# Two layers of a hybrid decoder in one kernel: the stationary tiles and the split weights at other SBUF addresses

## The chip, the cores and the metric

The kernel runs on one core of a Trainium2 chip. The metric is the device time of one execution in microseconds (us). Three runs of the kernel before took 2104.9, 2106.04 and 2107.2 us; the median is 2106.04 us. TensorE, VectorE, ScalarE and GpSimd are called PE, DVE, ACT and POOL, as in the profile; SP is the queue that starts the transfers.

## The reference

The input x has 256 positions of 2048 numbers. Each of the two layers does this:

```python
h = rmsnorm(x, norm_mix)
q, k, v, u_ssm, z_u, z_v = split(h @ w_in)          # 2048 -> 2816
y_attn = sliding_window_gqa(q, k, v, attn_sinks)    # 16 heads, window of 128
y_ssm  = s5_mixer(u_ssm, ...)                       # scan over positions, then GLU
y_gmlp = gmlp_mixer(z_u, z_v, ...)                  # gating in chunks of 128
y = concat(rmsnorm(y_attn), rmsnorm(y_ssm), rmsnorm(y_gmlp))
x = x + y @ w_out                                   # 2048 -> 2048
h = rmsnorm(x, norm_ffn)
x = x + (silu(h @ w_gate) * (h @ w_up)) @ w_down    # 2048 -> 5632 -> 2048
```

and a last RMSNorm ends it. All of it is float32. The products with `w_in`, `w_out`, `w_gate`, `w_up`, `w_down` and the GLU weight are called dense here; they are nearly all of the arithmetic.

## The kernel before

**Weights.** All dense weights lie in DRAM as one list of 684 halves of 128x1024 float32 (512 KB each), in the order of their use. `pump` (line 159 issues it) loads a half into one of five `raw` buffers. `split_hi` (line 168, ACT) rounds it to a tile `whi` of the type fp32r, and `split_lo` (line 178, DVE) puts the rest, raw minus whi, into a tile `wlo`; there are four buffers of each. So every weight is whi + wlo.

**Stationary tiles.** The activations are split in the same way and held transposed, ready to be loaded into the PE array as the stationary operand. `xh` and `xl` hold the two parts of the 2048 normalised inputs (16 blocks of 128 rows by 256 positions; the pair is called X). `ya` and `yb` hold blocks 0 to 7 and 8 to 15 of the input of `w_out` and `w_down`, each with both parts inside (Y). These are the four stationary tiles, each 16 KiB in a partition.

**The product.** `unit` takes one block k and, for each half m of the positions, issues three matmuls of 512 columns into one accumulator: xh with whi (line 260), xh with wlo (line 261), xl with whi (line 262). The trace names the moving tile first: `acc<-whi,xh` has whi moving and xh stationary. Every matmul comes with its own load of 128 stationary columns (LDWEIGHTS, engine PEld). A half of the weights serves 12 matmuls. `dense` runs over the blocks; after each `unit` pair it calls `tick`, which lets the waiting small jobs (attention, state space, transposes, evictions) put their instructions between the dense ones. The trace calls their PSUM tiles `side`.

**Order.** Per layer: `w_in` from X, `w_out` and the GLU product from Y, then the feed-forward part in three sets of four, four and three column groups: `w_gate` and `w_up` from X, `w_down` from Y. In `w_down` the blocks run from ya to yb and, for the next 512 output columns, again from ya to yb. The order on every engine is written out by the program itself (`manual_schedule`); pools only give out buffers and addresses.

**Addresses.** A pool lays its tiles out in the order in which their tags first appear, one pool behind the other. `xh` and `xl` (lines 953, 954) come from the pool `const`, everything else named here from the one pool `work`. Pools decide nothing but the address: a tag keeps its number of buffers wherever it lies.

Of the kernel before, what the change touches and what calls it, by code (L numbers as in the profile page):

```python
# [1 line left out]

# [8 lines left out]
F32R = mybir.dt.float32r  # L11
# [107 lines left out]
class Split:  # L119
    def __init__(self, parts):  # L120
        self.parts = parts

    def _at(self, i, k0, k1):
        hi, lo, base = self.parts[k0 // 8 if len(self.parts) > 1 else 0]
        return (hi, lo)[i][:, k0 - base:k1 - base]
# [3 lines left out]

    def lo(self, k0, k1):  # L130
        return self._at(1, k0, k1)


class Builder:
# [811 lines left out]
    def build(self):  # L946
        nc = self.nc
        dr = self.dr
        cst = self.const
        W = self.work  # L950

        self.x = cst.tile([128, 2, 2048], F32, name="x")
        xh = cst.tile([128, 16, 256], F32R, name="xh")
        xl = cst.tile([128, 16, 256], F32R, name="xl")
        self.X = Split([(xh, xl, 0)])
        self.Y = Split([None, None])
        self.ident = cst.tile([128, 128], F32, name="ident")
# [50 lines left out]
        for l in range(L):  # L1008
# [53 lines left out]
            for t in out_tiles():  # L1062
# [12 lines left out]
                f = n not in accs  # L1075
# [80 lines left out]
        for m in range(2):  # L1156
            r = nrm["rs"][:, m:m + 1]
            t = self.work.tile([128, 2], F32, tag="ms", name="ms", bufs=4)
# [13 lines left out]
def build_program(shapes):  # L1172
    nc = bacc.Bacc("TRN2", target_bir_lowering=False, num_devices=1, dynamic_dma_scratch_size=1024)
    dr = {n: nc.dram_tensor(n, s, F32, kind="ExternalInput").ap() for n, s in shapes.items()}
    dr["out"] = nc.dram_tensor("out", (2, 128, D), F32, kind="ExternalOutput").ap()
    with tile.TileContext(nc) as tc:
        with tc.tile_pool(name="const", bufs=1) as cst, tc.tile_pool(name="work", bufs=1) as wrk, \
                tc.tile_pool(name="ps", bufs=1, space=bass.MemoryType.PSUM) as ps, \
                tc.tile_pool(name="dram", bufs=1, space=bass.MemoryType.DRAM) as dram:
            with tc.manual_schedule():  # L1180
                b = Builder(nc, tc, (cst, wrk, ps, dram), dr)
                b.build()
    return nc, b

# [11 lines left out]
```

## Time and profile before

| | |
|---|---|
| median of three runs | 2106.04 us |
| profiled execution | 2106.98 us |
| its span, first to last instruction | 2105.1 us |
| PE busy | 2076.0 us (99%) |
| loads of stationary columns (PEld) | 1708.8 us (81%) |
| DVE busy | 1213.1 us (58%) |
| ACT busy | 969.4 us (46%) |
[...]

Matmuls are pipelined and their ends are modelled, so they overlap in the trace: one of 512 columns lasts near 390 ns, but the next starts some 230 ns after it. What a matmul costs in a row of matmuls is therefore the distance between two starts, not its duration.

### The profile page before, as it was taken

The page shows a single profiled execution, that of the slowest core. Times are in us where ns is not written, and L with a number is a line of the kernel's source. Part 1 is how long each engine was busy: PE and PEld are TensorE (multiplying, and loading weights), DVE is VectorE, ACT ScalarE, POOL GpSimd, SP SyncE. Part 2 cuts the span into 40 slices and gives each one's busy share as a digit, 9 for nine tenths or more (in the row PEclk, how much of TensorE's full clock was granted, in tenths as well). Part 3 has the DMA queues.
Part 4 walks back from the last instruction along what each step waited for, and adds up shares of the span by engine and source line. Part 5 has one row for each costly group of instructions (what it writes and reads, how often), then busy time and mean ns, then how long its engine had stood idle before and what let it go on. Part 6 is the DMA issues. An engine that isn't in the chain of part 4 may idle for free.

```text
span 2105.1 us, 25614 instructions
## 1 busy us (share of the span) xinstructions
PE 2076.0 (99%) x9728; PEld 1708.8 (81%) x9728; DVE 1213.1 (58%) x1625; ACT 969.4 (46%) x1289; POOL 204.4 (10%) x196
## 2 busy tenths in 40 slices
PE   8998999999999999999999999999999999999998
PEld 7788888888888888888888888888888888888886
DVE  6998765655555555444556795554454444554445
ACT  6555554444444443344455445544443444434443
POOL 0555004031312100000000010000000000000000
PEclk9998999999999999999999999999999999999999
DMA  7433455565656565555565455555555555555554
GB/s 243 166 128 133 140 180 190 185 212 189 220 189 214 185 210 190 190 183 188 180 215 179 152 187 174 180 189 181 188 183 191 187 184 186 187 191 183 187 193 140
DMA packets 105595, 387.98 MB, mean 184 GB/s; under 512 B 12288, under 2 KB 13056, under 8 KB 104192
## 3 DMA queue, kind: packets, MB, share of 16 engines
q1 hardware_dynamic: 105472, 386.35, 54.8%
q8 instruction: 76, 1.25, 0.2%
q14 instruction: 47, 0.39, 0.1%
HBM read 375.03 MB, written 11.27 MB: 184 GB/s over the span
## 4 chain that ended last, share of the span: by engine, by line
PE 95%; DVE 3%; issue 1%; ACT 0%; DMA 0%; SPq 0%; POOLq 0%; POOL 0%; ACTq 0%
PE acc L260 29%; PE acc L261 29%; PE acc L262 29%; PE side L324 2%; PE side L834 1%; DVE wlo L178 1%; PE side L606 1%; PE side L798 1%; DVE st L614 0%; PE side L566 0%; PE side L823 0%; PE side L644 0%; PE side L642 0%; PE side L639 0%; DMA x<-x 0%
## 5 line engine op out<-in xcount | busy, mean ns | idle before, releaser
L178 DVE TENSOR_TENSOR wlo<-raw,whi 128x1024 fp32r<-128x1024 f32 (+1 forms) x687 | 857.5, 1253 | 686.9 <-ACT whi L168 685.7
L168 ACT ACTIVATE whi<-raw 128x1024 fp32r<-128x1024 f32 (+1 forms) x687 | 725.3, 1057 | 1005.5 <-PE acc L262 943.8
L260 PE MATMUL acc<-whi,xh 128*128 128x512 f32 (+1 forms) x1792 | 711.4, 397 | 1.4 <-ACT whi L168 1.4
L261 PE MATMUL acc<-wlo,xh 128*128 128x512 f32 (+1 forms) x1792 | 701.6, 392 | 0.2 <-DVE wlo L178 0.2
L262 PE MATMUL acc<-whi,xl 128*128 128x512 f32 (+1 forms) x1792 | 701.3, 391 | 0.0
L262 PEld LDWEIGHTS acc<-whi,xl 128*128 128x128 f32 x1792 | 337.5, 188 | 77.4
L260 PEld LDWEIGHTS acc<-whi,xh 128*128 128x128 f32 x1792 | 337.9, 189 | 73.5 <-ACT whi L168 1.8
L261 PEld LDWEIGHTS acc<-wlo,xh 128*128 128x128 f32 x1792 | 338.0, 189 | 73.0 <-DVE wlo L178 1.0
L260 PE MATMUL acc<-whi,ya 128*128 128x512 f32 x512 | 204.6, 400 | 0.0
L262 PE MATMUL acc<-whi,ya 128*128 128x512 f32 x512 | 202.0, 395 | 0.0
L261 PE MATMUL acc<-wlo,ya 128*128 128x512 f32 x512 | 202.0, 394 | 0.0
L260 PE MATMUL acc<-whi,yb 128*128 128x512 f32 x448 | 176.6, 394 | 0.0
L262 PE MATMUL acc<-whi,yb 128*128 128x512 f32 x448 | 174.8, 390 | 0.0
L261 PE MATMUL acc<-wlo,yb 128*128 128x512 f32 x448 | 174.5, 390 | 0.0
L298 POOL TENSOR_TENSOR rs<-ms,nh 128x2 f32<-128x2 f32 (+1 forms) x12 | 12.2, 1014 | 1532.9 <-DVE ms L297 1413.6
L262 PEld LDWEIGHTS acc<-whi,ya 128*128 128x128 f32 x512 | 96.3, 188 | 22.7
L261 PEld LDWEIGHTS acc<-wlo,ya 128*128 128x128 f32 x512 | 96.5, 189 | 21.5
L260 PEld LDWEIGHTS acc<-whi,ya 128*128 128x128 f32 x512 | 96.5, 189 | 21.3
L262 PEld LDWEIGHTS acc<-whi,yb 128*128 128x128 f32 x448 | 84.1, 188 | 18.0
L260 PEld LDWEIGHTS acc<-whi,yb 128*128 128x128 f32 x448 | 84.1, 188 | 17.1
L261 PEld LDWEIGHTS acc<-wlo,yb 128*128 128x128 f32 x448 | 84.2, 188 | 17.0
L360 DVE SCALAR_TENSOR_TENSOR xl<-side,gains,xh 128x256 fp32r<-128x256 f32 x64 | 27.9, 479 | 45.6 <-ACT xh L358 45.5
(223 smaller groups left out, 1278.0 us busy)
## 6 DMA issues: line engine op xcount, KB each, us to landing
raw<-wts SPq DMA_DIRECT2D x684, 512.0 KB, 3.8
saved<-stash SPq DMA_DIRECT2D x4, 1792.0 KB, 6.5
stash<-saved SPq DMA_DIRECT2D x3, 1792.0 KB, 7.4
stashb<-saved SPq DMA_DIRECT2D x2, 1792.0 KB, 9.4
bc<-bc SPq DMA_DIRECT2D x8, 256.0 KB, 3.5
out<-x SPq DMA_DIRECT2D x8, 256.0 KB, 3.0
saved<-stashb SPq DMA_DIRECT2D x1, 1792.0 KB, 7.4
x<-x SPq DMA_DIRECT2D x3, 512.0 KB, 8.0
```

Of the source, the lines that this page charges most:

```text
L168: self.nc.scalar.activation(out=h[:, o:o + w], in_=self.raw[j][:, o:o + w], func=AF.Copy)
L178: self.nc.vector.tensor_tensor(out=o[:, i:i + w], in0=r[:, i:i + w], in1=self.hi[j][:, i:i + w], op=ALU.subtract)
L260: nc.tensor.matmul(out=o, lhsT=a, rhs=wh, start=first, stop=False)
L261: nc.tensor.matmul(out=o, lhsT=a, rhs=wl, start=False, stop=False)
L262: nc.tensor.matmul(out=o, lhsT=b, rhs=wh, start=False, stop=last)
L298: nc.gpsimd.tensor_tensor(out=out, in0=t, in1=self.nh[:, 0:w], op=ALU.pow)
L324: nc.tensor.transpose(ps[:, 256 * kk + 128 * m:256 * kk + 128 * m + 128], parts(2 * b + kk, m), self.ident)
L360: nc.vector.scalar_tensor_tensor(out=o, in0=src, scalar=gain[:, k:k + 1], in1=h.bitcast(F32), op0=ALU.mult, op1=ALU.subtract)
L606: nc.tensor.matmul(out=ps[:, 256 * o + 64 * g:256 * o + 64 * g + 64], lhsT=st[nm][:, 128 * g:128 * g + 128], rhs=U4[:, 4 * ct + g, :])
L798: nc.tensor.matmul(out=ps[:, nk * i:nk * i + nk], lhsT=qT[:, h0 + i], rhs=self.kT[:, j, cq, 0:nk], start=(j == 0), stop=(j == 1))
L834: nc.tensor.matmul(out=ps[:, 64 * i:64 * i + 64], lhsT=pT[:, 128 * (nb * i + b):128 * (nb * i + b) + 128], rhs=self.v[:, b, 64 * cq:64 * c ...
```

## The change

`const` gives up `xh` and `xl`, and the pool `work` becomes four pools, laid out one behind the other. A class `Homes` stands in for the pool and sends each tag to its pool: first everything that is not named, then `whi` and `wlo`, then the four stationary tiles, then a few tiles of the state space and gating parts.

```diff
+class Homes:
+    TAGS = (
+        (),
+        ('whi', 'wlo'),
+        ('xh', 'xl', 'ya', 'yb'),
+        ('stash', 'S', 'U4', 'st', 'wst', 'v', 'bb'),
+    )
+
+    def __init__(self, pools):
+        self.home = {t: p for ts, p in zip(self.TAGS, pools) for t in ts}
+        self.rest = pools[0]
+
+    def tile(self, shape, dtype, tag, name, bufs=1):
+        return self.home.get(tag, self.rest).tile(shape, dtype, tag=tag, name=name, bufs=bufs)
...
-        xh = cst.tile([128, 16, 256], F32R, name="xh")
-        xl = cst.tile([128, 16, 256], F32R, name="xl")
+        xh = W.tile([128, 16, 256], F32R, tag="xh", name="xh")
+        xl = W.tile([128, 16, 256], F32R, tag="xl", name="xl")
...
-        with tc.tile_pool(name="const", bufs=1) as cst, tc.tile_pool(name="work", bufs=1) as wrk, \
...
+            cst = pool("const")
+            homes = Homes([pool(f"work{i}") for i in range(len(Homes.TAGS))])
```

The instructions, their order on each engine and the semaphores that they wait for are the same in both programs; what differs is where the tiles lie. Addresses within a partition, as the two programs have them (each matmul loads 512 bytes of its stationary tile, at a multiple of 512 bytes from the tile's start):

| tile | before, bytes | before, KiB | after, bytes | after, KiB |
|---|---|---|---|---|
| x (residual stream) | 1152 | 1.1 to 17.1 | 1152 | 1.1 to 17.1 |
| xh | 17536 | 17.1 to 33.1 | 130816 | 127.75 to 143.75 |
| xl | 33920 | 33.1 to 49.1 | 147200 | 143.75 to 159.75 |
| yb | 151552 | 148.0 to 164.0 | 163584 | 159.75 to 175.75 |
| ya | 202112 | 197.4 to 213.4 | 179968 | 175.75 to 191.75 |
| raw, five | from 57984 | 56.6 to 76.6 | from 25216 | 24.6 to 44.6 |
| whi, four | from 80640 | 78.75 to 94.75 | from 98048 | 95.75 to 111.75 |
| wlo, four | from 97024 | 94.75 to 110.75 | from 114432 | 111.75 to 127.75 |
| t4, four (small jobs) | from 113408 | 110.75 to 126.75 | from 47872 | 46.75 to 62.75 |
| stash (state space) | 181632 | 177.4 to 191.4 | 198400 | 193.75 to 207.75 |

## Rows read from the trace of the kernel before

**Rows 1.** The page: busy time and share of the span, then instructions.
```profile
PE 2076.0 (99%) x9728; PEld 1708.8 (81%) x9728; DVE 1213.1 (58%) x1625; ACT 969.4 (46%) x1289; POOL 204.4 (10%) x196
```
**Rows 2.** The page: the chain that ended last, by engine and by line.
```profile
PE 95%; DVE 3%; issue 1%; ACT 0%; DMA 0%; SPq 0%; POOLq 0%; POOL 0%; ACTq 0%
PE acc L260 29%; PE acc L261 29%; PE acc L262 29%; PE side L324 2%; PE side L834 1%; DVE wlo L178 1%; PE side L606 1%; PE side L798 1%; DVE st L614 0%; PE side L566 0%; PE side L823 0%; PE side L644 0%; PE side L642 0%; PE side L639 0%; DMA x<-x 0%
```
**Rows 3.** Busy time by stage: us, engines (instructions), granted clock, DMA share, GB/s.
```profile
60.00:250.00 190.00, 178.55 (x1005) 154.73 (x1004) 165.17 (x353) 105.34 (x202) 77.48 (x77) 0.95 0.40 139
250.00:1100.00 850.00, 850.00 (x3800) 691.81 (x3799) 461.28 (x455) 381.71 (x449) 103.42 (x95) 1.00 0.58 195
1300.00:2050.00 750.00, 750.00 (x3298) 608.65 (x3297) 371.67 (x350) 317.69 (x343) 1.60 (x1) 1.00 0.57 187
...
552.20:563.30 11.10, 11.10 (x49) 9.03 (x48) 7.51 (x7) 4.25 (x4) 6.55 (x4) 1.00 0.81 287
...
872.50:922.30 49.80, 49.80 (x216) 40.38 (x215) 24.23 (x22) 20.25 (x20) 0.00 (x0) 1.00 0.57 190
```
**Rows 4.** Instructions of PE in order, 552 to 575 us: start, duration, what.
```profile
552.19 0.40 PE L260 MATMUL acc<-whi,ya 128*128 128x512 f32 x1
...
563.12 0.40 PE L262 MATMUL acc<-whi,ya 128*128 128x512 f32 x1
563.35 0.39 PE L260 MATMUL acc<-whi,yb 128*128 128x512 f32 x1
...
574.01 0.40 PE L262 MATMUL acc<-whi,yb 128*128 128x512 f32 x1
574.24 0.40 PE L260 MATMUL acc<-whi,ya 128*128 128x512 f32 x1
```
**Rows 5.** Groups of PE, 552.20 to 563.30 us: count, busy us, mean ns.
```profile
L260 PE MATMUL acc<-whi,ya 128*128 128x512 f32 x16 | 6.3, 395 | 0.0
```
**Rows 6.** The same groups, 563.40 to 574.20 us.
```profile
L260 PE MATMUL acc<-whi,yb 128*128 128x512 f32 x16 | 6.2, 389 | 0.0
```
**Rows 7.** Instructions of PE in order, 872 to 923 us.
```profile
872.39 0.40 PE L260 MATMUL acc<-whi,xh 128*128 128x512 f32 x1
...
922.36 0.39 PE L262 MATMUL acc<-whi,xl 128*128 128x512 f32 x1
922.59 0.60 PE L324 MATMUL side<-ident,t 128*128 128x128 f32 x4
```
**Rows 8.** Groups of PE, 872.50 to 922.30 us.
```profile
L260 PE MATMUL acc<-whi,xh 128*128 128x512 f32 x72 | 28.4, 395 | 0.0
```
**Rows 9.** Instructions that read yb: duration ns min/median/max, first and last start.
```profile
L260 PE MATMUL acc<-whi,yb x448: 389/389/486, 249.7 to 2095.0; 128*128 128x512 f32 x150
L260 PE MATMUL side<-whi,yb x16: 389/389/498, 244.1 to 1279.7; 128*128 128x512 f32 x16
```
**Rows 10.** Groups of PE, 250 to 2100 us, shapes kept apart.
```profile
L260 PE MATMUL acc<-whi,xh 128*128 128x512 f32 x1568 | 625.5, 399 | 0.0
L260 PE MATMUL acc<-whi,ya 128*128 128x512 f32 x480 | 191.3, 399 | 0.0
L260 PE MATMUL acc<-whi,yb 128*128 128x512 f32 x448 | 176.6, 394 | 0.0
L324 PE MATMUL side<-ident,t 128*128 128x128 f32 x208 | 30.8, 272 | 0.0
```
**Rows 11.** Groups of PE, 0 to 250 us, shapes kept apart.
```profile
L260 PE MATMUL acc<-whi,xh 128*128 128x512 f32 x160 | 67.6, 423 | 1.4 <-ACT whi L168 1.4
L260 PE MATMUL acc<-whi,ya 128*128 128x512 f32 x32 | 13.3, 414 | 0.0
```
**Rows 12.** Groups of the whole span, shapes kept apart: mean ns, idle time before.
```profile
L178 DVE TENSOR_TENSOR wlo<-raw,whi 128x1024 fp32r<-128x1024 f32 x681 | 853.7, 1258 | 686.9 <-ACT whi L168 685.7
L168 ACT ACTIVATE whi<-raw 128x1024 fp32r<-128x1024 f32 x681 | 721.8, 1060 | 1004.6 <-PE acc L262 943.8 <-issue 30.8 <-ACT whi L168 7.7
L260 PE MATMUL acc<-whi,xh 128*128 128x512 f32 x1728 | 693.1, 401 | 1.4 <-ACT whi L168 1.4
```

More of the change, by code (lines that the diff above doesn't have):

```diff
@@ L1 @@
+import contextlib
 import math
@@ L1176, in build_program @@
     with tile.TileContext(nc) as tc:
-        with tc.tile_pool(name="const", bufs=1) as cst, tc.tile_pool(name="work", bufs=1) as wrk, \
-                tc.tile_pool(name="ps", bufs=1, space=bass.MemoryType.PSUM) as ps, \
-                tc.tile_pool(name="dram", bufs=1, space=bass.MemoryType.DRAM) as dram:
+        with contextlib.ExitStack() as st:
+            pool = lambda name, **kw: st.enter_context(tc.tile_pool(name=name, bufs=1, **kw))
+            cst = pool("const")
+            homes = Homes([pool(f"work{i}") for i in range(len(Homes.TAGS))])
+            ps = pool("ps", space=bass.MemoryType.PSUM)
+            dram = pool("dram", space=bass.MemoryType.DRAM)
             with tc.manual_schedule():
-                b = Builder(nc, tc, (cst, wrk, ps, dram), dr)
+                b = Builder(nc, tc, (cst, homes, ps, dram), dr)
                 b.build()
```

## The prediction

> **What bounds the kernel now.** I read the busy shares first: PE is busy for 2076.0 of 2105.1 us [rows 1]. A busy PE need not be a PE at its peak, so next comes the chain that ended last: 95% of it is PE, and 87% is the three dense lines [rows 2]. The stages say the same: from 250 to 1100 us and from 1300 to 2050 us PE is busy without a gap at full granted clock, while DVE stands at 54% (461.28 of 850), ACT at 45% and the transfers at 58% [rows 3]. Only before 250 us does PE wait: from 60 to 250 us it is busy for 178.55 of 190 us, DVE for 165.17 (87%), and the granted clock is 0.95 [rows 3]. So for some 1800 us the time is the number of matmuls times the distance from one start to the next, and nothing else.
>
> The third view is that distance, from instructions in order of time. In one `w_down` stage the blocks run through ya and then yb. The first ya matmul starts at 552.19 us, the first yb matmul at 563.35, the next ya matmul at 574.24 [rows 4]; between them lie 16 matmuls on each of three lines, 48 in all [rows 5, 6]. That is 11.16 us / 48 = 232.5 ns on ya and 10.89 us / 48 = 226.9 ns on yb. The instruction, its 512 columns, the moving tiles and the clock are the same; what differs is the stationary tile. X behaves like ya: from 872.39 to 922.59 us [rows 7] stand 72 matmuls on each line [rows 8], so 50.20 us / 216 = 232.4 ns. It isn't one lucky stretch: of the 448 yb matmuls of line 260 the shortest and the median last 389 ns, and the same holds for the 16 that write another PSUM tile [rows 9], while the pure stretch of X averages 395 [rows 8].
>
> Now the addresses. xh and xl lie at 17 to 49 KiB, ya at 197 to 213 KiB, yb at 148 to 164 KiB. The slow tiles lie on both sides of the fast one. Line 260, with whi moving, lasts as long over X as over ya, and yb is fast under the same moving buffers; so the moving tile doesn't make the difference. I read it as a property of where the stationary tile lies. The change puts all four between 127.75 and 191.75 KiB, and keeps whi and wlo between 64 and 128 KiB, where they are now.
>
> **The change part by part.** No instruction, order or wait is added or removed, so the sum has only durations in it.
>
> *X moves to 127.75 KiB.* After 250 us there are 1568 matmuls of 512 columns on line 260 with xh [rows 10], so 4704 on three lines. If each costs what yb's cost, the gain is 4704 x (232.4 - 226.9) = 25.9 us.
>
> *ya moves from 197 to 175.75 KiB.* 480 on line 260 after 250 us [rows 10], 1440 in all, at 232.5 - 226.9 = 5.6 ns: 8.1 us.
>
> *yb moves from 148 to 159.75 KiB.* It is fast now and stays so: 0. If it loses its place, 448 x 3 + 16 x 3 = 1392 matmuls [rows 9] pay 5.6 ns: 7.8 us lost.
>
> *Before 250 us* there are (160 + 32) x 3 = 576 such matmuls [rows 11], worth 0 to 3.2 us at 5.5 ns. DVE is the busier partner there, at 87% against 54% later, so a quicker PE mostly waits sooner; I take 1 us.
>
> *Switches.* The matmul during which a load from another place runs seems to stay slow: the last yb before ya takes 574.24 - 574.01 = 0.23 us, and so does the last xl before the transposes [rows 4, 7]. Those small jobs stay elsewhere. The 208 transposes of one kind come in fours [rows 7, 10], 52 entries at 5.5 ns: 0.3 us, for all kinds some 0.5 us off the gain.
>
> *raw, whi, wlo and the small tiles move too.* ACT's split takes 1060 ns on the mean and DVE's 1258, with 1004.6 and 686.9 us of idle time before them [rows 12]. In the trace both are spread evenly over their buffers' addresses, from 57 to 111 KiB; the new ones are not sampled. Their cover is the half's 12 matmuls: 12 x 226.9 ns = 2.72 us, against 1.26 us of DVE. Even a tenth more would hide after 250 us. So 0; in the early stage, where DVE is short, 1% on its 165.17 us [rows 3] would be 1.7 us either way. Transfers move 512 KB a half, and their share rises from 0.58 to 0.60.
>
> The sum is 25.9 + 8.1 + 1.0 - 0.5 = 34.5 us. The profiled execution took 2106.98 us, 1.9 us more than its span; less 34.5 that is 2072.5, and the median of the runs lies 0.9 us lower. I predict 2072 us.
>
> The distance between 5.0 and 7 ns bounds it from rows: with all matmuls that follow a small job counted in, line 260's mean is 399 on xh and ya against 394 on yb after 250 us [rows 10], 6144 x 5 = 30.7 us; over the whole span xh has 401 [rows 12], 7 ns above 394, and 7 x 6720 = 47 us would be the most, if each line gained like line 260 and the early waits fell as well. The clean starts lie nearer the lower end, so I keep 34.5; the forecast's own range is 2063 to 2079 us.
>
> [...]
>
> **The rivals.**
>
> *The fast place is yb's own (slower).* In this trace two properties of yb go together: it lies between 128 and 192 KiB, and it starts at 151552 bytes, a whole multiple of 4096. The three slow tiles start 128 or 384 bytes past a multiple of 512; after the change all four start 256 past one. If the fine alignment to 512 or more decides, or the exact 16 KiB, no tile is fast afterwards and yb pays its 7.8 us: 2106 + 8 = 2114 us. It decides if yb's matmuls stand at 232 ns afterwards. Against it: the new starts are multiples of 256, as yb's is and the slow ones aren't, and so only an alignment that counts from 512 bytes up, or a span narrower than the change's, would take the gain away. A chance of 0.11.
>
> *Part of the span is fast.* xh, at 127.75 to 143.75 KiB, lies wholly outside what yb has sampled. If the fast span begins at 144 KiB, two of X's three loads stay slow, and the third is between two switches, each 0.23 us [rows 4]: X gains nothing, ya gains its 8.1 us, 2098 us. If instead only the part above 164 KiB were slow, X would gain and ya not: 2080, about 2084 with half of yb's place lost. Together 0.07, spread from 2080 to 2100.
>
> *The address is invisible.* Then yb is fast because of what runs beside it. For it: the transfers ran at 287 GB/s beside ya's stretch, with POOL at work for 6.55 of 11.10 us [rows 3]. Against it: X's 216 matmuls, with POOL idle and 190 GB/s [rows 3], stand at the same 232.4 ns. 2106 us, 0.05. [...]
>
> **How the numbers follow.** Forecast 0.77, slower 0.11, part 0.07, invisible 0.05. A difference under 0.2% (4.2 us) can't be told from no change here. Faster takes the forecast and nearly all of the partial cases: 0.83; same 0.06; slower 0.11. The range takes in the forecast's own 2063 to 2079 and the better part of the partial cases: 2063 to 2090 us.
>
> **What would show it.** In the profile after, a pure stretch of X and one of ya should each show 227 ns from start to start, medians of 389 ns, and no slow matmul where ya and yb meet. The stage from 250 to 1100 us should hold the same work in some 833 us, and DVE and ACT keep 1258 and 1060 ns. The second step fails if xh is slow and ya fast (part of the span), all of it if yb reads 232 (its own place). The forecast is wrong with right reasons if the distances are 227 and PE shows new waits for whi or wlo after 250 us.

## The result, and the profile after

The changed kernel takes 2071.23 us (median of four runs, 2070.05 to 2073.87), against 2106.27 us for the kernel before (2104.9 to 2107.2). The ratio is 0.9836, with a 95% interval of 0.9819 to 0.9853: 35 us less. The forecast was 2072 us, in a range of 2063 to 2090.

The page of the changed kernel begins so; the third line answers to [rows 1].

```profile
span 2072.0 us, 25614 instructions
...
PE 2041.6 (99%) x9728; PEld 1708.3 (82%) x9728; DVE 1210.9 (58%) x1625; ACT 969.9 (47%) x1289; POOL 206.1 (10%) x196
```

The counts are those of before. The busy time that is gone is PE's: 34.4 us, where the other engines differ by 2.2 us or less, and the span is 33.1 us shorter. The chain that ended last is still PE's:

```profile
PE 94%; DVE 4%; issue 1%; ACT 0%; DMA 0%; SPq 0%; POOLq 0%; POOL 0%; ACTq 0%; DVEq 0%
```

Next the instructions of PE in order of time (start, duration, what), for the same pair of `w_down` runs as in [rows 4]. The dense lines are now 279 to 281.

```profile
547.11 0.39 PE L279 MATMUL acc<-whi,ya 128*128 128x512 f32 x1
...
557.77 0.39 PE L281 MATMUL acc<-whi,ya 128*128 128x512 f32 x1
557.99 0.39 PE L279 MATMUL acc<-whi,yb 128*128 128x512 f32 x1
...
568.65 0.39 PE L281 MATMUL acc<-whi,yb 128*128 128x512 f32 x1
568.87 0.39 PE L279 MATMUL acc<-whi,ya 128*128 128x512 f32 x1
```

The 48 matmuls on ya take 10.88 us and the 48 on yb 10.88, 226.7 ns each; ya's were 232.5 ns before. The last matmul of each run, next to the other tile, takes 0.22 us where it took 0.23. A pure stretch of X stands in the same view:

```profile
861.15 0.39 PE L279 MATMUL acc<-whi,xh 128*128 128x512 f32 x1
...
910.12 0.60 PE L343 MATMUL side<-ident,t 128*128 128x128 f32 x4
```

Between the two lie the 216 matmuls of [rows 7] and [rows 8]: 48.97 us / 216 = 226.7 ns, where it was 232.4. The instructions that read each tile (duration as min/median/max, then first and last start), which answer to [rows 9]:

```profile
L279 PE MATMUL acc<-whi,xh x1792: 278/389/794, 10.0 to 1994.5; 128*128 128x512 f32 x193, 128*128 128x256 f32 x7
...
L279 PE MATMUL acc<-whi,ya x512: 388/389/486, 213.9 to 2059.1; 128*128 128x512 f32 x171
...
L279 PE MATMUL acc<-whi,yb x448: 389/389/486, 250.0 to 2061.8; 128*128 128x512 f32 x150
```

All three tiles have the median that only yb had, 389 ns. The last column of times says where the gain lies: the first yb matmul starts at 250.0 us, after 249.7 before, so no gain shows up to there; the last one starts 33.2 us earlier. And the groups of line 279 after 250 us (count, busy us, mean ns), which answer to [rows 10], and the two splits over the whole span, which answer to [rows 12]:

```profile
L279 PE MATMUL acc<-whi,xh 128*128 128x512 f32 x1568 | 618.0, 394 | 0.0
...
L279 PE MATMUL acc<-whi,ya 128*128 128x512 f32 x480 | 188.9, 393 | 0.0
...
L279 PE MATMUL acc<-whi,yb 128*128 128x512 f32 x448 | 176.4, 394 | 0.0
```

```profile
L197 DVE TENSOR_TENSOR wlo<-raw,whi 128x1024 fp32r<-128x1024 f32 x681 | 851.7, 1255 | 658.8 <-ACT whi L187 657.9
L187 ACT ACTIVATE whi<-raw 128x1024 fp32r<-128x1024 f32 x681 | 722.4, 1061 | 969.3 <-PE acc L281 919.2 <-issue 27.8 <-ACT whi L187 8.0
```

The splits cost what they cost before (1258 and 1060 ns). Their idle time shrank by 28 and 35 us. For most of it DVE waits for ACT's part, 657.9 us where it was 685.7, and ACT for a matmul of PE, 919.2 us where it was 943.8.

### The profile page after: what moved, and what is told of

Same layout as the page of the kernel before. It is cut to its first block, busy times and chain, and to the rows that moved or that the text cites. A ratio compares the mean times of both kernels' runs of the same rounds, so it can differ in the third digit from the quotient of the medians.

```text
span 2072.0 us, 25614 instructions
## 1 busy us (share of the span) xinstructions
PE 2041.6 (99%) x9728; PEld 1708.3 (82%) x9728; DVE 1210.9 (58%) x1625; ACT 969.9 (47%) x1289; POOL 206.1 (10%) x196
## 4 chain that ended last, share of the span: by engine, by line
PE 94%; DVE 4%; issue 1%; ACT 0%; DMA 0%; SPq 0%; POOLq 0%; POOL 0%; ACTq 0%; DVEq 0%
PE acc L279 29%; PE acc L281 29%; PE acc L280 29%; PE side L343 2%; DVE wlo L197 1%; PE side L853 1%; PE side L625 1%; PE side L817 1%; DVE st L633 0%; PE side L585 0%; PE side L842 0%; PE side L663 0%; PE side L661 0%; DMA raw<-wts 0%; PE side L658 0%
## 5 line engine op out<-in xcount | busy, mean ns | idle before, releaser
L197 DVE TENSOR_TENSOR wlo<-raw,whi 128x1024 fp32r<-128x1024 f32 (+1 forms) x687 | 855.6, 1250 | 658.9 <-ACT whi L187 657.9
L187 ACT ACTIVATE whi<-raw 128x1024 fp32r<-128x1024 f32 (+1 forms) x687 | 725.8, 1058 | 971.1 <-PE acc L281 919.2
L279 PE MATMUL acc<-whi,xh 128*128 128x512 f32 (+1 forms) x1792 | 704.2, 393 | 1.9 <-ACT whi L187 1.9
L281 PE MATMUL acc<-whi,xl 128*128 128x512 f32 (+1 forms) x1792 | 693.1, 387 | 0.0
L280 PE MATMUL acc<-wlo,xh 128*128 128x512 f32 (+1 forms) x1792 | 692.6, 387 | 0.0
L279 PE MATMUL acc<-whi,ya 128*128 128x512 f32 x512 | 202.0, 394 | 0.0
L281 PE MATMUL acc<-whi,ya 128*128 128x512 f32 x512 | 199.5, 390 | 0.0
```

The source lines that it names most:

```text
L187: self.nc.scalar.activation(out=h[:, o:o + w], in_=self.raw[j][:, o:o + w], func=AF.Copy)
L197: self.nc.vector.tensor_tensor(out=o[:, i:i + w], in0=r[:, i:i + w], in1=self.hi[j][:, i:i + w], op=ALU.subtract)
L279: nc.tensor.matmul(out=o, lhsT=a, rhs=wh, start=first, stop=False)
L280: nc.tensor.matmul(out=o, lhsT=a, rhs=wl, start=False, stop=False)
L281: nc.tensor.matmul(out=o, lhsT=b, rhs=wh, start=False, stop=last)
```

## The experiments

The forecast rests on a reading: a stationary tile is quick because of the place where it lies. The theory *span* says that the place is 128 to 192 KiB. The theory *start* says that it is the start of the tile, a multiple of 256 bytes or not. The first two kernels each move one tile of 128 bytes, so that the two theories part, and the third leaves the model out.

**The stationary pair X 128 bytes later, in its old place.** In the kernel before:

```diff
+        self.sinks = cst.tile([128, L, 16], F32, name="sinks")
         xh = cst.tile([128, 16, 256], F32R, name="xh")
         xl = cst.tile([128, 16, 256], F32R, name="xl")
...
-        self.sinks = cst.tile([128, L, 16], F32, name="sinks")
```

Expected:

> The kernel before with one 128-byte tile (sinks) moved ahead of xh, so that xh and xl start 128 bytes later, at multiples of 256 bytes (17664 and 34048), still far below 128 KiB; whi, wlo, ya and yb keep their addresses. Theory span (a stationary tile is quick where it lies between 128 and 192 KiB): X stays at 232.4 ns from start to start, 2106 us. Theory start (it is quick where it starts at a multiple of 256 bytes, as yb did and the three slow tiles did not): X falls to 227 ns, 4704 x 5.5 ns = 26 us less, 2080 us.

Measured: 2078.36 us, ratio 0.9874 (0.986 to 0.9889). This is start's number and not span's. The groups of PE from 250 to 2100 us in this kernel:

```profile
L260 PE MATMUL acc<-whi,xh 128*128 128x512 f32 x1568 | 617.8, 394 | 0.0
...
L260 PE MATMUL acc<-whi,ya 128*128 128x512 f32 x480 | 191.4, 399 | 0.0
...
L260 PE MATMUL acc<-whi,yb 128*128 128x512 f32 x445 | 175.5, 394 | 0.0
```

X, at 17 KiB, is as quick as yb, 394 ns on the mean; ya, untouched, keeps its 399 ns. The span theory falls here, although its number was right.

**Everything 128 bytes earlier.** In the changed kernel:

```diff
-        ('stash', 'S', 'U4', 'st', 'wst', 'v', 'bb'),
+        ('stash', 'S', 'U4', 'st', 'wst', 'v', 'bb', 'smh'),
```

Expected:

> The changed kernel with one 128-byte tile (smh) moved from the first pool to the last, so that whi, wlo and the four stationary tiles start 128 bytes earlier: the stationary tiles lie 128 bytes off a multiple of 256 (as the slow tiles of before did), at 127.6 to 191.6 KiB. Theory span: all stay at 227 ns, 2071 us. Theory start: all four are slow at 232.4 ns, 2071 + 35 + 8 = 2114 us.

Measured: 2070.29 us, ratio 0.9839 (0.9822 to 0.9855). This is span's number and not start's. The groups of PE from 250 to 2100 us:

```profile
L279 PE MATMUL acc<-whi,xh 128*128 128x512 f32 x1568 | 617.7, 394 | 0.0
...
L279 PE MATMUL acc<-whi,ya 128*128 128x512 f32 x480 | 188.8, 393 | 0.0
...
L279 PE MATMUL acc<-whi,yb 128*128 128x512 f32 x444 | 174.8, 394 | 0.0
```

So neither theory of the stationary tile alone holds both results. What the first kernel changed and the second did not is the distance between the stationary and the moving tile: in the second, whi and wlo moved along.

**A map without the model.** The core of the kernel, with `r` the thirteen tiles ra to rm, 16 KiB each:

```python
for s in TILES:              # stationary
    for m in TILES:          # moving
        for q in range(16):
            nc.tensor.matmul(**mm(q, s, m, 0, 0, False, False))    # line 47: no offset
# lines 51, 55, 59, 63: stationary, moving, both 128 bytes late, both 256 bytes late
```

Expected:

> Nothing of the model is computed: thirteen fp32r tiles ra to rm lie at 16, 32, ... 208 KiB, each 16 KiB long, filled with part of x, and TensorE runs 16 matmuls of 512 columns for every pair of a stationary tile and a moving tile, with no other engine at work; then for 7 stationary and 5 moving tiles again with the stationary, the moving or both operands 128 bytes later, and with both 256 bytes later. Theory span: rh, ri, rj and rk (128 to 192 KiB) as stationary show about 227 ns from start to start and 389 ns of duration, all others about 232 and 393, whatever the moving tile and whatever the offset. Theory start: all tiles show 227 with no offset and with 256 bytes, and 232 where the stationary operand is 128 bytes late. A third theory, pair: what counts is the stationary tile against the moving one, and the quick pairs follow the distance between them or their 64 KiB blocks, so that 128 to 192 KiB is quick under a moving tile in 64 to 128 KiB and not under one elsewhere.

It took 1171.15 us. Busy time of PE and PEld by pass, for the lines 47, 51, 55, 59 and 63 in turn (stretch, its length, busy us and matmuls):

```profile
0.00:1169.00 1169.00, 613.08 (x2704) 507.51 (x2704) 1.00 0.01 3
0.00:1169.00 1169.00, 130.29 (x560) 105.52 (x560) 1.00 0.01 3
0.00:1169.00 1169.00, 130.82 (x560) 105.14 (x560) 1.00 0.01 3
0.00:1169.00 1169.00, 127.14 (x560) 105.11 (x560) 1.00 0.01 3
0.00:1169.00 1169.00, 127.10 (x560) 105.11 (x560) 1.00 0.01 3
```

Divided by the matmuls: 226.7 ns over all 169 pairs of places, 232.7 with the stationary operand 128 bytes late, 233.6 with the moving one late, and 227.0 with both late, by 128 or by 256 bytes. Of the 169 pairs the costliest has 3.8 us of busy time for its 16 matmuls, 389 ns each; with the moving operand 128 bytes late all 35 pairs have 3.9 us, and 394 or 395 ns each. So no span and no pair of blocks is slow. Only the third theory, pair, is left, and not in the form in which it was written: neither blocks of 64 KiB nor large distances count, but a small distance between the two operands. The map has only 0 and 128 bytes of it; that it counts modulo 256 is read from the kernel before, where yb and the first whi lie 277 x 256 bytes apart (151552 and 80640) and take 226.9 ns. Once the tiles are filled the program gives the other engines nothing to do until the last matmul, and the transfers' share is 0.01, so contention with them isn't needed for the 6 ns.

**The moving tiles alone 128 bytes earlier.** In the changed kernel:

```diff
-        ('whi', 'wlo'),
+        ('whi', 'wlo', 'smh'),
```

Expected:

> The changed kernel with the 128-byte tile smh moved behind wlo, so that whi and wlo start 128 bytes earlier while the four stationary tiles keep the addresses of the changed kernel (130816 to 196352). Theory pair (what counts is the distance between the stationary and the moving operand's start, modulo 256 bytes): all dense matmuls are slow at 232 to 234 ns, yb's too, so at least 2071 + (6720 + 1392) x 5.6 ns = 2116 us, slower than the kernel before. Theories span and start: the stationary tiles have not moved, 227 ns, 2071 us.

Measured: 2113.93 us, ratio 1.0042 (1.0026 to 1.0059): slower than the kernel before, with every stationary tile where the changed kernel has it. Groups of PE from 250 to 2100 us:

```profile
L279 PE MATMUL acc<-whi,xh 128*128 128x512 f32 x1568 | 625.5, 399 | 0.0
...
L279 PE MATMUL acc<-whi,ya 128*128 128x512 f32 x480 | 191.3, 399 | 0.0
...
L279 PE MATMUL acc<-whi,yb 128*128 128x512 f32 x441 | 175.9, 399 | 0.0
```

All three are at 399 ns, yb too. The expectation of 2116 us or more was 2 us too high; its direction and the place are right.

**The pools in another order.** In the changed kernel:

```diff
     TAGS = (
+        ('xh', 'xl', 'ya', 'yb'),
         (),
         ('whi', 'wlo'),
-        ('xh', 'xl', 'ya', 'yb'),
-        ('stash', 'S', 'U4', 'st', 'wst', 'v', 'bb'),
+        ('stash', 'S', 'U4', 'st', 'wst', 'v', 'bb', 'smh'),
     )
...
-        self.rest = pools[0]
+        self.rest = pools[1]
```

Expected:

> The changed kernel with its four pools in another order: the stationary tiles at 24.6 to 88.6 KiB, whi and wlo at 159.6 to 191.6 KiB, all of them 128 bytes past a multiple of 256, so that the distances between them are multiples of 256 bytes. Theory pair: 227 ns everywhere, 2071 us. Theory span: no stationary tile is in the quick span, 232 ns, 2114 us. Theory start (multiples of 256): 2114 us as well.

Measured: 2070.71 us, ratio 0.9836 (0.9822 to 0.9851), the changed kernel's own ratio, with the stationary tiles below 89 KiB and the weights above 159. Two of the groups of PE from 250 to 2100 us:

```profile
L279 PE MATMUL acc<-whi,xh 128*128 128x512 f32 x1568 | 617.7, 394 | 0.0
...
L279 PE MATMUL acc<-whi,ya 128*128 128x512 f32 x480 | 188.8, 393 | 0.0
```

**The distance in small steps.** Again without the model:

```python
for o in (0,) + LATE + (0,):     # line 54: bytes by which the stationary operand is late
    for q in range(48):
        nc.tensor.matmul(**ops(S[o], o // 4, M[0], 0))
# line 57: the moving operand late; 60, 63: 256, 384 columns; 66: bf16; 69: fp32
```

Expected:

> Nothing of the model is computed: every tile starts at a multiple of 512 bytes, and TensorE runs 48 fp32r matmuls of 512 columns for each of 16 stationary tiles whose operand starts 0 to 448 bytes late (late128b is 128 bytes late), then with the moving operand late (mov32b and so on), then 256 and 384 columns, then bf16 (half), then fp32 (wide). Theory pair with a period of 256: 0 and 256 bytes late take 227 ns, 128 and 384 take 233, the values between are not known; late and mov by the same bytes mirror each other. If the cost followed the distance in finer steps, some value other than 0 and 256 would lie below 227 or well above 234. With 256 columns the kernel's rows show 120 ns at a distance of 128 bytes already, so little or no cost is expected there.

It took 625.97 us. The instructions of PE in order of time, merged where they are alike; from the start of one row to the start of the next are 48 matmuls (47 of the 48 bf16 matmuls have a record; the fp32 rows are 24 matmuls, each with two records):

```profile
41.70 11.32 PE L54 MATMUL acc<-mov0b,late4b 128*128 128x512 f32 x48
52.86 11.36 PE L54 MATMUL acc<-mov0b,late16b 128*128 128x512 f32 x48
64.06 11.35 PE L54 MATMUL acc<-mov0b,late32b 128*128 128x512 f32 x48
75.25 11.36 PE L54 MATMUL acc<-mov0b,late64b 128*128 128x512 f32 x48
86.45 11.40 PE L54 MATMUL acc<-mov0b,late96b 128*128 128x512 f32 x48
97.69 11.36 PE L54 MATMUL acc<-mov0b,late112b 128*128 128x512 f32 x48
108.88 11.37 PE L54 MATMUL acc<-mov0b,late128b 128*128 128x512 f32 x48
120.08 11.37 PE L54 MATMUL acc<-mov0b,late144b 128*128 128x512 f32 x48
131.29 11.36 PE L54 MATMUL acc<-mov0b,late160b 128*128 128x512 f32 x48
142.48 11.16 PE L54 MATMUL acc<-mov0b,late192b 128*128 128x512 f32 x48
153.48 11.36 PE L54 MATMUL acc<-mov0b,late224b 128*128 128x512 f32 x48
164.67 11.04 PE L54 MATMUL acc<-mov0b,late256b 128*128 128x512 f32 x48
175.55 11.36 PE L54 MATMUL acc<-mov0b,late320b 128*128 128x512 f32 x48
186.75 11.32 PE L54 MATMUL acc<-mov0b,late384b 128*128 128x512 f32 x48
197.91 11.16 PE L54 MATMUL acc<-mov0b,late448b 128*128 128x512 f32 x48
208.91 11.06 PE L54 MATMUL acc<-mov0b,late0b 128*128 128x512 f32 x48
219.81 11.04 PE L57 MATMUL acc<-mov0b,late0b 128*128 128x512 f32 x48
230.69 11.37 PE L57 MATMUL acc<-mov32b,late0b 128*128 128x512 f32 x48
241.89 11.16 PE L57 MATMUL acc<-mov64b,late0b 128*128 128x512 f32 x48
252.89 11.32 PE L57 MATMUL acc<-mov128b,late0b 128*128 128x512 f32 x48
264.04 11.36 PE L57 MATMUL acc<-mov192b,late0b 128*128 128x512 f32 x48
275.24 11.09 PE L57 MATMUL acc<-mov256b,late0b 128*128 128x512 f32 x48
286.16 5.91 PE L60 MATMUL acc<-mov0b,late0b 128*128 128x256 f32 x48
291.91 5.84 PE L60 MATMUL acc<-mov0b,late4b 128*128 128x256 f32 x48
297.59 5.84 PE L60 MATMUL acc<-mov0b,late16b 128*128 128x256 f32 x48
...
377.26 8.50 PE L63 MATMUL acc<-mov0b,late0b 128*128 128x384 f32 x48
385.60 8.56 PE L63 MATMUL acc<-mov0b,late4b 128*128 128x384 f32 x48
...
410.66 8.55 PE L63 MATMUL acc<-mov0b,late64b 128*128 128x384 f32 x48
419.05 8.64 PE L63 MATMUL acc<-mov0b,late96b 128*128 128x384 f32 x48
427.53 8.69 PE L63 MATMUL acc<-mov0b,late112b 128*128 128x384 f32 x48
436.06 8.61 PE L63 MATMUL acc<-mov0b,late128b 128*128 128x384 f32 x48
...
486.64 8.64 PE L63 MATMUL acc<-mov0b,late320b 128*128 128x384 f32 x48
495.12 8.61 PE L63 MATMUL acc<-mov0b,late384b 128*128 128x384 f32 x48
...
511.89 10.53 PE L66 MATMUL acc<-halfmov,half0b 128*128 128x512 bf16 x47
522.26 10.52 PE L66 MATMUL acc<-halfmov,half32b 128*128 128x512 bf16 x47
532.62 10.52 PE L66 MATMUL acc<-halfmov,half64b 128*128 128x512 bf16 x47
...
574.06 20.76 PE L69 MATMUL acc<-widemov,wide0b 128*128 128x512 f32 x48
594.66 20.76 PE L69 MATMUL acc<-widemov,wide128b 128*128 128x512 f32 x48
```

At 0 the distance from start to start is 10.90 us / 48 = 227 ns, and 256 bytes late it is the same (10.88). 4 bytes late it is 11.16 / 48 = 232.5, 16 bytes late 11.20 / 48 = 233. Then there is one value that was not expected: 192 bytes late costs 11.00 / 48 = 229, and so do 448 late and a moving operand 64 bytes late, which is the same distance modulo 256. So at 512 columns the period of 256 bytes stands (64 and 320 bytes late take 11.20 us each, 128 and 384 late 11.20 and 11.16), and the two operands mirror each other (moving 32 late 11.20 and stationary 224 late 11.19, moving 192 late and stationary 64 late 11.20 each); but the cost is not two-valued. No distance tried lies below the 10.88 us.

## Why the prediction was right, and where its reason was wrong

The time was right, and so were the two large terms. The step on which they rest was wrong, the sentences "so the moving tile doesn't make the difference. I read it as a property of where the stationary tile lies." It is a property of the pair: 226.7 ns in the map with both operands at the same remainder, 232.7 and 233.6 with one of them 128 bytes late. All eight buffers of whi and wlo lie 4096 bytes apart, so in the kernel before they have one and the same remainder modulo 256 bytes: 0. A trace with one moving remainder can't show that the moving tile matters. xh and xl were 128 past a multiple of 256, ya too, and yb was at 0. That is what told yb from the others, and not its 64 KiB. The change gives all of whi, wlo, xh, xl, ya and yb the remainder 0, because the sizes of the tiles ahead of them happen to add up so; the kernel with smh in the last pool has 128 for all of them and is as quick (2070.29 us), and the one with only whi and wlo at 128 is slow (2113.93 us). The prediction did see that the new starts are multiples of 256, but held it only against a rival and made it no condition of the gain. By the reason that it gives, the right remainders, and with them the right time, were luck.

*What bounds the kernel.* Right: PE's distance from start to start is the time after 250 us (PE is busy for 850.00 us of the 850 up to 1100 us in the changed kernel too), and it fell from 232.4 and 232.5 to 226.7 ns where the runs are pure. The dense matmuls that took 850 us from the first on yb (249.7 us) take 833.4 now, as forecast.

*X, 25.9 us.* Right in size, and shown by itself: the kernel that moves X by 128 bytes in its old place is 26.9 us quicker (2105.26 to 2078.36).

*ya, 8.1 us.* Between that kernel and the changed one, which differ in ya's remainder and in the places of the tiles, lie 7.1 us (2078.36 to 2071.23), or 8.1 by what each gained on the runs of the kernel before taken beside it (26.9 and 35.0). ya alone was not tried. The forecast took 5.6 ns from a pure run.

*yb, 0, or 7.8 us if lost.* Both ends were seen: 0 in the changed kernel, a median of 389 ns as before; with the moving tiles off, 8.8 us above the kernel before (2113.93 against 2105.13).

*Before 250 us, 1 us.* Not shown either way. The first yb matmul starts at 250.0 us in the changed kernel and at 249.7 in the kernel before, but at 247.4 in the kernel where everything lies 128 bytes earlier, which is as quick, and at 247.5 in the one where the moving tiles alone do, which is slow. A term of 1 us is lost in that spread; that DVE holds this stretch was not tried.

*Switches, 0.5 us off the gain.* Rows to 0.01 us hardly tell 227 from 232 ns, but the trace keeps whole nanoseconds. Before, the last yb matmul ahead of ya took 232 ns (574.007 to 574.239 us), and it has a load from another remainder beside it; now it takes 226 (568.648 to 568.874). That load isn't the whole of it: the last ya matmul ahead of yb, with a yb load beside it, took 232 as well (563.117 to 563.349). The entries into small jobs were not tried apart.

*The splits and the other tiles, 0.* Right: 1255 and 1061 ns.

The rival "the fast place is yb's own" was nearer to the cause than the forecast: it named the fine alignment. Its outcome was wrong, since it looked at the stationary start alone and from 512 bytes up. The 8 us that it priced came when the moving tiles were put 128 bytes off. The rival "part of the span" fell with the span, and "the address is invisible" with the map, where 6 ns remain (226.7 against 232.7) though PE alone has work.

For bf16, at six offsets (10.36 or 10.37 us for 48 matmuls), and for fp32, at two (20.76 us for 24), the address makes no difference in the rows. For fp32r with 512 columns it does: from 227 ns with the two operands at the same remainder to 232.5 with the stationary one 4 bytes off and 233 with it 16 bytes off. Why it does was not shown; the runs show the pattern and its price.

## What to carry to other kernels

When a trace shows one tile quicker than its likes, list all that sets it apart, the remainder of its address among it, and the address of the operand that it is used with; here a shift of 128 bytes separated the theories in one run. For fp32r matmuls of 512 columns, give the stationary and the moving tiles the same remainder modulo 256 bytes: with it the matmuls here took some 227 ns, without it 229 to 234. A tile of 128 bytes allocated ahead of one of them was worth 1.3% (X, 2105.26 to 2078.36 us) to 2% (whi and wlo, 2071.23 to 2113.93). A right time doesn't prove the reason: the layout with the same aim and one tile of 128 bytes elsewhere, behind wlo, was slower than the kernel before (2113.93 us).

## What the runs showed of the hardware that was not expected

- The price depends on the number of columns. At 256 columns a misaligned pair is not slower: 5.75 us for 48 at distance 0 and 5.68 at 4 bytes, 120 and 118 ns, with the sixteen offsets between 5.64 and 5.76 us, where 512 columns rise from 227 to 232.5. 384 columns lie between: 8.34 us / 48 = 174 ns at distance 0 and 8.53 / 48 = 178 at 112 bytes. There 64 and 320 bytes late don't cost the same (8.39 and 8.48 us), so the period of 256 bytes is shown for 512 columns alone.
- It belongs to fp32r alone among the types tried. bf16 takes 10.37 and 10.36 us / 48 = 216 ns at 0 and at 32 bytes, and 10.36 at the four other offsets, and fp32 20.60 us / 24 = 858 ns at 0 (429 for each of the two records of a matmul); its rows at 0 and at 128 bytes last the same 20.76 us, and no other distance was tried for it.
- So even an aligned fp32r matmul of 512 columns stands 11 ns above a bf16 one (227 against 216 ns).
